# A mask added by a product and six modulation chunks moved to VectorE, in an attention and MLP layer

## The chip, the core and the metric

The kernel runs on one core of a Trainium2 chip. The metric is the device time of one execution in microseconds (us), taken as the median of several runs. In the profile, TensorE's products are rows of PE and its weight loads rows of PEld; VectorE is DVE, ScalarE is ACT, GpSimd is POOL, and SP is the queue that issues most transfers.

## What is computed

One transformer layer on 256 positions of width 2048, in float32, for one sequence. What matters here, cut from the reference:

```python
mod = silu(c) @ mod_w + mod_b                      # 2048 x 12288, a single row
sh_m, sc_m, g_m, sh_f, sc_f, g_f = split(mod, 6)
h = x * (1 + sc_m) + sh_m
q, k, v = split(h @ w_qkv + b_qkv)                 # 32 query heads, 8 key/value heads of 64
s = (rope(q) @ rope(k).T) * 64 ** -0.5
s = where(abs(kpos - qpos) <= 128, s, -inf)
m = maximum(max(s), sink)
p = exp(s - m); p = p / (sum(p) + exp(sink - m))
x = layer_norm(alpha * x + (1 + g_m) * ((p @ v) @ w_o + b_o))
h = x * (1 + sc_f) + sh_f
y = square(relu(h @ w1 + b1)) @ w2 + b2
x = layer_norm(alpha * x + (1 + g_f) * y)
```

With 256 positions there are two query blocks t of 128. Each sees both key blocks. In its own key block nothing is masked. In the other one the window of 128 cuts a triangle off: so the mask has one corner of 128 x 128 that isn't all zero for each t.

## The kernel before

**Numbers.** Full-precision products are made of three products of rounded float32 (float32r): high x high, high x low, low x high (`mm3`, lines 561 to 564; three such products are called a triple below). So every weight tile is loaded once (`raw`, 1 MB), rounded by ScalarE to its high part (`wh`, line 300), and VectorE subtracts to get the low part (`wl`, line 251). Scores, transposes and values are done in plain float32, which the trace shows as two instructions for each product.

**Stages.** The weights stream in the order of their use. First comes the projection to q, k and v (up to some 160 us), beside it the modulation's first part. Then comes the attention stage (`for n in range(21)`): sixteen score sets n = 0 to 15. A set is four query heads of one query block t (n = 4j + 2t + rh). In iteration n the kernel issues the scores of set n, the values of an earlier pair of sets, and a block of weight products: the last parts of q, k and v for small n, then the output projection (`project`). Inside the block stand the transposes of the probabilities of set n - 1 (`probs_T`) and the normalising of set n. Then comes the MLP, which is most of the span and which the change doesn't touch.

**A score set** (`scores`, line 758). Four products of 256 columns (line 775) go to two PSUM banks, two heads in each. VectorE runs `tensor_tensor_reduce` once for each head (line 782): it adds the mask's 256 columns, changes the sign, writes that back to PSUM and reduces the minimum, with the negated sink as the start, into a column of `nm`. In the trace each is a CUSTOM_DVE_ANT_0 and a short DVE_READ_ACCUMULATOR2_ANT. A small addition makes `es` for the sink's term (line 786). ScalarE takes the exponential of each head, with sums (line 791). The mask is written once by GpSimd (`masks`, line 122), as two pieces of 256 columns.

**Modulation.** A chunk is 1 MB of the modulation's weights (`Mod.step`). It goes one of two ways. On TensorE it is `quad`s (line 364): products whose fixed operand has 32 equal columns of the conditioning vector, four of them in the four 32-wide column strips. A chunk of the gate (`m_gm`, width 512) is four products of 512 columns, a chunk of `m_ff` (width 256) eight of 256. On VectorE it is two multiply-adds over 1024 columns (line 404; the first of a group is line 402), into two tiles (for `m_ff`, two into one tile). At a group's end the VectorE part is reduced by four products with ones (line 364, in = `onesf`) on top of TensorE's part. Which chunks go where is written by hand: the lists behind `m_mix`, `m_ff` and `m_gm` (lines 469 to 472).

**What sets the order.** The loads' order and the pace are tables. Within them a scheduler orders the instructions of each engine by the priorities in `AHEAD`, so a change of work moves other instructions too. Once built, each engine runs its queue in order.

Of the kernel before, what the change touches and what calls it, by code (L numbers as in the profile page):

```python
# [21 lines left out]
NT = S // 128  # L22
NK = D // 128
# [6 lines left out]
NEG = -1.0e30  # L30
# [3 lines left out]
FFG = (4, 4, 4, 4)  # L34
# [28 lines left out]
def hybrid_kernel(ctx: ExitStack, tc: tile.TileContext, a, out: bass.AP):  # L63
    nc = tc.nc
    cst = ctx.enter_context(tc.tile_pool(name="cst", bufs=1))
# [38 lines left out]
    onesf = cst.tile([128, 128], F32, name="onesf")  # L104
    nc.vector.memset(onesf, 1.0)
    nc.vector.tensor_copy(onesr, onesf)
    eps = cst.tile([128, 1], F32, name="eps")
    nc.vector.memset(eps, LN_EPS)
    both = cst.tile([128, 2], F32, name="both")
# [10 lines left out]
    fixed = sml.tile([128, 1024], F32, name="sc", bufs=1)  # L120

    def masks():
        msk = fixed[:, :512].rearrange("p (t k) -> p t k", t=NT)
        nc.gpsimd.memset(msk, 0.0)
        nc.gpsimd.affine_select(out=msk[:, 0, 128:], in_=msk[:, 0, 128:], compare_op=OP.is_ge, fill=NEG, base=0,
                                pattern=[[-1, 128]], channel_multiplier=1)
        nc.gpsimd.affine_select(out=msk[:, 1, :128], in_=msk[:, 1, :128], compare_op=OP.is_ge, fill=NEG, base=0,
                                pattern=[[1, 128]], channel_multiplier=-1)
        return msk


    def rotary_tables():
# [327 lines left out]
    def groups(src, sizes, dves):  # L460
        out, c0, k0 = [], 0, 0
        for nk, dve in zip(sizes, dves):
            n = 2 * nk
            out.append((Mod([src[c0 + i] for i in range(n)], 64 * nk, dve), k0, nk))
            c0 += n
            k0 += nk
        return out

    m_mix = groups(a["modm"], MIXG, [(), (), (), (), (1,), (), (0, 4, 5, 6, 7), (3, 5, 6)])
    m_ff = groups(a["modf"], FFG, [(0, 3, 4, 7), (0, 1, 3, 4, 5, 6), (3, 4), (0, 1, 2, 3, 4, 5, 6, 7)])  # L470
    m_gm = Mod([a["modgm"][i] for i in range(NK)], 512, (3, 4, 5, 7, 9, 10, 12, 14), a["modgmb"])
    m_gf = Mod([a["modgf"][i] for i in range(NK)], 512, range(NK), a["modgfb"])

    scm = cst.tile([128, NK], F32, name="scm")
# [208 lines left out]
    for tok in STEPS.split():  # L683
        n = int(tok[1:])
        if tok[0] == "v":
            S.vecs(n)
        elif tok[0] == "i":
            idle(n)
        elif tok[0] == "p":
            S.pace = n  # L690
        elif tok[0] == "n":
            S.nh = n
        elif tok[0] == "l":
            S.nl = n
        elif tok[0] == "M":
            modulated(n)
            if n == 0:
                msk = masks()
# [62 lines left out]
    def scores(n):  # L761

        j, rh, t = n // 4, n % 2, n % 4 // 2

        def of(x):
            return x.rearrange("p (g r i) -> p g r i", r=2, i=2)[:, 2 * j:2 * j + 2, rh]

        pss = [psa.tile([128, 512], F32, name="pa").rearrange("p (i k) -> p i k", i=2) for _ in range(2)]
        nm = sml.tile([128, 4], F32, name="nm")
        for i in range(2):  # L770
            x = (2 * rh + i) * 256 + t * 128
            for s in range(2):
                p = slice(64 * s, 64 * s + 64)
                with first("scores"):
                    nc.tensor.matmul(pss[s][:, i], qT[j][p, x:x + 128], kT[p, j * 256:j * 256 + 256],  # L775
                                     start=True, stop=True)
        with first("softmax"):
            for s in range(2):

                for i in range(2):  # L780
                    h = 4 * (2 * j + s) + 2 * rh + i
                    nc.vector.tensor_tensor_reduce(out=pss[s][:, i], in0=pss[s][:, i], in1=msk[:, t], scale=-1.0,
                                                   scalar=nsnk[:, h:h + 1], op0=OP.add, op1=OP.min,
                                                   accum_out=nm[:, 2 * s + i:2 * s + i + 1])
            es = sml.tile([128, 4], F32, name="es")
            nc.vector.tensor_tensor(es.rearrange("p (s i) -> p s i", s=2), nm.rearrange("p (s i) -> p s i", s=2),
                                    of(snk), op=OP.add)
            P = g4()
            sm = sml.tile([128, 4], F32, name="sm")
            for r in range(4):  # L790
                nc.scalar.activation(P[:, r * 256:r * 256 + 256], pss[r // 2][:, r % 2], AF.Exp, scale=-1.0,
                                     bias=nm[:, r:r + 1], accum_out=sm[:, r:r + 1])
            nc.scalar.activation(es, es, AF.Exp)
        PS[n] = P, sm, es
# [188 lines left out]
    for n in range(21):  # L983
        j, i = n // 4, n % 4
# [574 lines left out]
```

## Time and profile before

| | us |
|---|---|
| median of 3 runs (lowest, highest) | 1066.85 (1065.62, 1068.74) |
| span of the profiled execution | 1064.5 |
| its time in the list of runs | not given on its own; the lowest run is 1065.62 |
| TensorE busy with products | 1051.1 |
| VectorE busy | 964.0 |
| ScalarE busy | 625.4 |

Read it so: the share of busy time is an average over stages. TensorE's rows overlap, since one product starts before the end of the one before it, so the cost of a product is the distance to the next start. Buffer numbers are left out of names: `pa`, `pt` and `pm` are PSUM banks, `g` and `g4b` general tiles of 1024 columns. The granted clock of TensorE is 1.000 for the execution.

### The profile page before, as it was taken

To read this page: it belongs to the slowest core of one execution; us is meant where nothing else is said; L and a number is where in the kernel's file an instruction comes from. 1 tells how busy PE (TensorE), PEld (TensorE's weight loads), DVE (VectorE), ACT (ScalarE), POOL (GpSimd) and SP (SyncE) were. 2 spreads that over 40 slices of the span, in tenths; PEclk is the share of its full clock that TensorE was granted. 3 is DMA by queue.
4 is the path that set the end of the run, shared out by engine and by line. 5 is a ranking of instruction groups with operands and counts; after the bars stand their busy time and mean duration, and the time that the engine had idled before them with its cause. 6 is when DMAs were issued, how large, how long until landed. Compare 5 with 4: busy or idle time off the path is not lost.

```text
span 1064.5 us, 16048 instructions
## 1 busy us (share of the span) xinstructions
PE 1051.1 (99%) x6172; PEld 854.8 (80%) x6172; DVE 964.0 (91%) x1448; ACT 625.4 (59%) x986; POOL 27.6 (3%) x54
## 2 busy tenths in 40 slices
PE   9999899999999999999999999999999999999998
PEld 7677677666677899988888888888888888888886
DVE  4689899989999898999989999899899997999998
ACT  5433347776772637664367777447777446777740
POOL 1000000001000000000000000000000001000000
PEclk9999999999999999999999999999999999999999
DMA  9999997799965897538945654974564793465742
GB/s 383 425 423 426 426 427 300 286 384 354 393 244 199 330 383 294 219 121 312 384 176 194 237 187 171 358 312 163 194 237 164 285 358 136 164 237 200 251 182 79
DMA packets 43516, 292.72 MB, mean 275 GB/s; under 512 B 5152, under 2 KB 5280, under 8 KB 9648
## 3 DMA queue, kind: packets, MB, share of 16 engines
q1 hardware_dynamic: 39456, 279.85, 67.5%
q0 software_dynamic: 3232, 10.50, 3.1%
q10 hardware_dynamic: 752, 1.35, 0.4%
q8 instruction: 48, 0.79, 0.3%
q14 instruction: 28, 0.23, 0.1%
HBM read 289.57 MB, written 2.11 MB: 274 GB/s over the span
## 4 chain that ended last, share of the span: by engine, by line
PE 94%; DVE 3%; ACT 1%; DMA 1%; issue 0%; DVEq 0%; ACTq 0%
PE pa L1195 17%; PE pa L562 15%; PE pa L564 15%; PE pa L563 15%; PE pa L1197 9%; PE pm L364 4%; PE pa L1169 3%; PE pa L1168 3%; PE pa L1167 3%; PE pa L775 2%; PE pt L564 2%; PE pt L563 2%; PE pt L562 2%; PE pa L836 1%; PE pt L819 1%; PE pa L672 1%
## 5 line engine op out<-in xcount | busy, mean ns | idle before, releaser
L300 ACT CAST wh<-raw 128x1024 fp32r<-128x1024 f32 (+1 forms) x332 | 333.8, 1016 | 251.0 <-PE pa L564 100.2
L251 DVE TENSOR_TENSOR wl<-raw,wh 128x1024 fp32r<-128x1024 f32 (+1 forms) x332 | 386.0, 1177 | 47.4 <-ACT wh L300 44.1
L562 PE MATMUL pa<-wh,g 128*128 128x512 f32 (+1 forms) x611 | 242.8, 399 | 4.8 <-ACT g L585 4.8
L563 PE MATMUL pa<-wl,g 128*128 128x512 f32 (+1 forms) x611 | 238.1, 390 | 0.0
L564 PE MATMUL pa<-wh,g 128*128 128x512 f32 (+1 forms) x611 | 237.3, 390 | 0.2 <-DVE g L587 0.2
L1195 PE MATMUL pa<-g,wh 128*128 128x512 f32 x768 | 191.5, 391 | 0.0
L1195 PEld LDWEIGHTS pa<-g,wh 128*128 128x128 f32 x768 | 140.6, 188 | 28.2 <-issue 0.8
L562 PEld LDWEIGHTS pa<-wh,g 128*128 128x128 f32 x611 | 114.7, 188 | 41.1 <-ACT g L585 6.4
L564 PEld LDWEIGHTS pa<-wh,g 128*128 128x128 f32 x611 | 114.7, 188 | 26.5 <-issue 1.6
L563 PEld LDWEIGHTS pa<-wl,g 128*128 128x128 f32 x611 | 114.9, 188 | 23.0 <-DVE scm L445 0.4
L1197 PEld LDWEIGHTS pa<-g,wl 128*128 128x128 f32 x768 | 104.8, 190 | 7.5
L1197 PE MATMUL pa<-g,wl 128*128 128x256 f32 x768 | 107.1, 282 | 0.0
L404 DVE SCALAR_TENSOR_TENSOR g<-raw,cact,g 128x1024 f32<-128x1024 f32 (+1 forms) x69 | 86.2, 1257 | 0.8 <-DMA raw<-in_modm 0.4
L1167 PE MATMUL pa<-g,wh 128*128 128x256 f32 x240 | 67.8, 285 | 0.2 <-ACT wh L300 0.2
L1169 PE MATMUL pa<-g,wh 128*128 128x256 f32 x240 | 67.6, 285 | 0.0
L1168 PE MATMUL pa<-g,wl 128*128 128x256 f32 x240 | 67.5, 285 | 0.0
L251 DVE TENSOR_TENSOR raw<-raw 128x1024 fp32r<-128x1024 f32 x54 | 65.6, 1221 | 0.0
L300 ACT CAST raw<-raw 128x1024 fp32r<-128x1024 f32 x54 | 56.0, 1045 | 8.2 <-DVE raw L262 4.4
L1168 PEld LDWEIGHTS pa<-g,wl 128*128 128x128 f32 x240 | 45.8, 192 | 0.7 <-issue 0.4
L1167 PEld LDWEIGHTS pa<-g,wh 128*128 128x128 f32 x240 | 45.9, 192 | 0.5 <-ACT wh L300 0.4
L1169 PEld LDWEIGHTS pa<-g,wh 128*128 128x128 f32 x240 | 45.8, 192 | 0.1
L605 DVE TENSOR_TENSOR g<-g,pa 128x512 f32<-128x512 f32 x60 | 39.3, 682 | 6.9 <-PE pa L564 6.6
(250 smaller groups left out, 1364.0 us busy)
## 6 DMA issues: line engine op xcount, KB each, us to landing
raw<-in_w1b SPq DMA_DIRECT2D x48, 1024.0 KB, 6.8
raw<-in_modm SPq DMA_DIRECT2D x32, 1024.0 KB, 12.6
raw<-in_modf SPq DMA_DIRECT2D x32, 1024.0 KB, 7.0
raw<-in_w SPq DMA_DIRECT2D x32, 1024.0 KB, 7.2
raw<-in_w2s SPq DMA_DIRECT2D x27, 1024.0 KB, 5.6
raw<-in_wqkv SPq DMA_DIRECT2D x24, 1024.0 KB, 14.2
raw<-in_modgm SPq DMA_DIRECT2D x16, 1024.0 KB, 7.3
raw<-in_wo SPq DMA_DIRECT2D x16, 1024.0 KB, 7.3
```

The lines of the kernel that those rows point to most:

```text
L251: self.pinned(nc.vector.tensor_sub(l[:, :w], r, f32(self.hs[n])[:, :w]))
L300: self.pinned(nc.scalar.copy(h[:, :s.shape[-1]], s))
L364: i = nc.tensor.matmul(self.ps[32 * j:32 * j + 32, :w], lhsT[j] if type(lhsT) is list else lhsT, rhs[j], start=self.first, stop=stop)
L404: nc.vector.scalar_tensor_tensor(p[:, :e], s, cact[:, kt:kt + 1], p[:, :e], op0=OP.mult, op1=OP.add)
L562: nc.tensor.matmul(ps, xh, wh, start=start, stop=False)
L563: nc.tensor.matmul(ps, xh, wl, start=False, stop=False)
L564: S.prev = nc.tensor.matmul(ps, xl, wh, start=False, stop=stop).ins
L1167: nc.tensor.matmul(o, wh(w, 128), hh, start=new, stop=False)
L1168: nc.tensor.matmul(o, wl(w, 128), hh, start=False, stop=False)
L1169: nc.tensor.matmul(o, wh(w, 128), hl, start=False, stop=end)
L1195: nc.tensor.matmul(ps, wh(k, 128), ff_in(k), start=k == 0, stop=False)
L1197: nc.tensor.matmul(ps[:, :256], wl(k, 128), ff_in(k)[:, :256], start=False, stop=k == NK - 1)
```

## The change

The mask's corner is now stored rounded, beside a rounded identity matrix, in a new tile `rounded`. ScalarE makes the two copies, next to the start of the kernel. In each score set, two products with the identity (one for each bank, 2 x 128 columns) add the corner onto the half of the scores that it belongs to, for both heads of the bank at once. VectorE then takes one maximum over 256 scores for the two heads of a bank (`tensor_reduce`, negated), so two instructions in a set instead of four, and a small one combines all four with the negated sink. Scores are no longer written back by VectorE, and their sign stays, so the exponential's scale of -1 goes.

Six more modulation chunks are summed on VectorE: one each of `m_ff`'s first two groups, and chunks 6, 11, 13 and 15 of the gate `m_gm`. To make room in SBUF, the buffer for GpSimd's transfer descriptors is set to 8192 bytes.

```diff
+    rounded = cst.tile([128, 512], F32R, name="rounded")
...
     def masks():
-        msk = fixed[:, :512].rearrange("p (t k) -> p t k", t=NT)
-        nc.gpsimd.memset(msk, 0.0)
-        nc.gpsimd.affine_select(out=msk[:, 0, 128:], in_=msk[:, 0, 128:], compare_op=OP.is_ge, fill=NEG, base=0,
-                                pattern=[[-1, 128]], channel_multiplier=1)
...
+        corner = fixed[:, :256].rearrange("p (t k) -> p t k", t=NT)
+        nc.gpsimd.memset(corner, 0.0)
+        for t, step in enumerate((-1, 1)):
+            nc.gpsimd.affine_select(out=corner[:, t], in_=corner[:, t], compare_op=OP.is_ge, fill=NEG, base=0,
+                                    pattern=[[step, 128]], channel_multiplier=-step)
+        nc.scalar.copy(rounded[:, :256], fixed[:, :256])
+        nc.scalar.copy(rounded[:, 256:384], ident)
+        return rounded[:, :256].rearrange("p (t k) -> p t k", t=NT), rounded[:, 256:384]
...
-    m_ff = groups(a["modf"], FFG, [(0, 3, 4, 7), (0, 1, 3, 4, 5, 6), (3, 4), (0, 1, 2, 3, 4, 5, 6, 7)])
-    m_gm = Mod([a["modgm"][i] for i in range(NK)], 512, (3, 4, 5, 7, 9, 10, 12, 14), a["modgmb"])
+    m_ff = groups(a["modf"], FFG, [(0, 2, 3, 4, 7), (0, 1, 2, 3, 4, 5, 6), (3, 4), (0, 1, 2, 3, 4, 5, 6, 7)])
+    m_gm = Mod([a["modgm"][i] for i in range(NK)], 512, (3, 4, 5, 6, 7, 9, 10, 11, 12, 13, 14, 15), a["modgmb"])
...
                     nc.tensor.matmul(pss[s][:, i], qT[j][p, x:x + 128], kT[p, j * 256:j * 256 + 256],
-                                     start=True, stop=True)
+                                     start=i == 0, stop=False)
+        far = slice(128 - 128 * t, 256 - 128 * t)
+        for s in range(2):
+            with first("scores"):
+                nc.tensor.matmul(pss[s][:, :, far], eye, msk[:, t, None, :].to_broadcast([128, 2, 128]),
+                                 start=False, stop=True)
         with first("softmax"):
             for s in range(2):
-
-                for i in range(2):
-                    h = 4 * (2 * j + s) + 2 * rh + i
-                    nc.vector.tensor_tensor_reduce(out=pss[s][:, i], in0=pss[s][:, i], in1=msk[:, t], scale=-1.0,
-                                                   scalar=nsnk[:, h:h + 1], op0=OP.add, op1=OP.min,
-                                                   accum_out=nm[:, 2 * s + i:2 * s + i + 1])
+                nc.vector.tensor_reduce(out=nm[:, 2 * s:2 * s + 2], in_=pss[s], axis=AX.X, op=OP.max, negate=True)
             es = sml.tile([128, 4], F32, name="es")
-            nc.vector.tensor_tensor(es.rearrange("p (s i) -> p s i", s=2), nm.rearrange("p (s i) -> p s i", s=2),
-                                    of(snk), op=OP.add)
+            nm3 = nm.rearrange("p (s i) -> p s i", s=2)
+            nc.vector.tensor_tensor(nm3, nm3, of(nsnk), op=OP.min)
+            nc.vector.tensor_tensor(es.rearrange("p (s i) -> p s i", s=2), nm3, of(snk), op=OP.add)
...
-                nc.scalar.activation(P[:, r * 256:r * 256 + 256], pss[r // 2][:, r % 2], AF.Exp, scale=-1.0,
+                nc.scalar.activation(P[:, r * 256:r * 256 + 256], pss[r // 2][:, r % 2], AF.Exp,
                                      bias=nm[:, r:r + 1], accum_out=sm[:, r:r + 1])
...
-    nc = bacc.Bacc("TRN2", target_bir_lowering=False, num_devices=1)
+    nc = bacc.Bacc("TRN2", target_bir_lowering=False, num_devices=1, dynamic_dma_scratch_size=8192)
```

The scheduler moves other instructions too. Two places matter to the prediction. In the new kernel the line numbers are higher by two or three.

The first place is VectorE's queue at score set 5. Before, with `pa` the scores, `nm` the maxima, `g_1524` and `g_1525` the two halves of the gate's sum:

```order
L840 TENSOR_TENSOR g_1896<-pa,g_1895 128x512
L782 ISA pa,nm<-pa,sc,nsnk 128x256
L782 ISA nm 128x1
L782 ISA pa,nm<-pa,sc,nsnk 128x256
L782 ISA nm 128x1
L782 ISA pa,nm<-pa,sc,nsnk 128x256
L782 ISA nm 128x1
L782 ISA pa,nm<-pa,sc,nsnk 128x256
L782 ISA nm 128x1
L251 TENSOR_TENSOR wl<-raw,wh 128x1024
L786 TENSOR_TENSOR es<-nm,pack 128x4
L404 SCALAR_TENSOR_TENSOR g_1524<-raw,cact,g_1524 128x1024
```

Before set 5, the value remainder (line 840) stands ahead of the scores' instructions. Now, the same engine and place, where `g_1527` and `g_1528` are the gate's sum:

```order
L406 SCALAR_TENSOR_TENSOR g_1527<-raw,cact,g_1527 128x1024
L786 TENSOR_REDUCE nm<-pa 128x2 x2
L843 TENSOR_TENSOR g_1900<-pa,g_1899 128x512
L789 TENSOR_TENSOR nm<-nm,nsnk 128x4
L406 SCALAR_TENSOR_TENSOR g_1528<-raw,cact,g_1528 128x1024
L790 TENSOR_TENSOR es<-nm,pack 128x4
L253 TENSOR_TENSOR wl<-raw,wh 128x1024 x2
L406 SCALAR_TENSOR_TENSOR g_1527<-raw,cact,g_1527 128x1024
L406 SCALAR_TENSOR_TENSOR g_1528<-raw,cact,g_1528 128x1024
L803 TENSOR_TENSOR rs<-sm,es 128x4
```

Two maxima stand where four pairs stood. Other work (a value remainder, a chunk's half) stands between the maxima and the small instructions that depend on them, and more chunk halves follow.

The second place is TensorE's queue between score sets 6 and 7, at the end of the gate's group. `pm` is the modulation's bank. Before, first the gate's last chunk with its reduction, and then, four triples later, the values and scores:

```order
L562 MATMUL pa<-wh,g_1895 128x512
L563 MATMUL pa<-wl,g_1895 128x512
L564 MATMUL pa<-wh,g_1896 128x512
L364 MATMUL pm<-raw,cact 32x512 x4
L364 MATMUL pm<-g_1524,onesf 32x512 x2
L364 MATMUL pm<-g_1525,onesf 32x512 x2
L819 MATMUL pt<-ident,g_2104 128x128 x8
```

The reduction follows directly on the last chunk, as one run of eight 32-wide products. The values and scores of the same iteration:

```order
L564 MATMUL pa<-wh,g_1896 128x512
L364 MATMUL pm<-raw,cact 32x256 x16
L836 MATMUL pa<-g_2158,g_330 64x512 x2
L836 MATMUL pa<-g_2159,g_330 64x512 x2
L775 MATMUL pa<-g_1589,g_1963 128x256 x4
L562 MATMUL pa<-wh,g_1895 128x512
```

They are runs of sixteen, four and four. Now the same engine and place:

```order
L566 MATMUL pa<-wh,g_1900 128x512
L839 MATMUL pa<-g_2161,g_333 64x512 x2
L366 MATMUL pm<-g_1527,onesf 32x512 x2
L839 MATMUL pa<-g_2162,g_333 64x512
L366 MATMUL pm<-g_1528,onesf 32x512 x2
L839 MATMUL pa<-g_2162,g_333 64x512
L777 MATMUL pa<-g_1592,g_1968 128x256 x2
L366 MATMUL pm<-raw,cact 32x256 x8
L777 MATMUL pa<-g_1592,g_1968 128x256 x2
L782 MATMUL pa<-rounded 128x2x128 x2
L822 MATMUL pt<-ident,g_2218 128x128 x8
```

The reduction has moved in among the value products, in two pieces, and eight modulation products stand in the middle of the scores. The new corner products (line 782 there) close the score set.

More of the change, by code (lines that the diff above doesn't have):

```diff
@@ L122, in masks @@
     def masks():
-        msk = fixed[:, :512].rearrange("p (t k) -> p t k", t=NT)
-        nc.gpsimd.memset(msk, 0.0)
-        nc.gpsimd.affine_select(out=msk[:, 0, 128:], in_=msk[:, 0, 128:], compare_op=OP.is_ge, fill=NEG, base=0,
-                                pattern=[[-1, 128]], channel_multiplier=1)
-        nc.gpsimd.affine_select(out=msk[:, 1, :128], in_=msk[:, 1, :128], compare_op=OP.is_ge, fill=NEG, base=0,
-                                pattern=[[1, 128]], channel_multiplier=-1)
-        return msk
+        corner = fixed[:, :256].rearrange("p (t k) -> p t k", t=NT)
[6 more added lines that the diff above has]
+        return rounded[:, :256].rearrange("p (t k) -> p t k", t=NT), rounded[:, 256:384]
     def rotary_tables():
@@ L697, in hybrid_kernel @@
             if n == 0:
-                msk = masks()
+                msk, eye = masks()
             if n == 2:
```

## The prediction

> **What bounds the kernel now.** I read the page first: the span, the engines' shares and the chain that ended last.
>
> ```profile
> span 1064.5 us, 16048 instructions
> PE 1051.1 (99%) x6172; PEld 854.8 (80%) x6172; DVE 964.0 (91%) x1448; ACT 625.4 (59%) x986; POOL 27.6 (3%) x54
> PE 94%; DVE 3%; ACT 1%; DMA 1%; issue 0%; DVEq 0%; ACTq 0%
> ```
>
> TensorE is on the chain for 94% of the span, so what the change puts on or takes off its queue counts almost fully, if TensorE gets what it waits for on time. VectorE, at 91%, is the engine that could fail to deliver. Where the change lies in time is told by line 782, the mask-and-maximum instruction that it removes (its view gives durations min/median/max, first and last start). The next rows are the busy time of each engine in that stretch (columns: stretch, length, then PE, PEld, DVE, ACT and POOL with counts, granted clock, DMA share, GB/s), and VectorE's for line 782 alone.
>
> ```profile
> L782 DVE CUSTOM_DVE_ANT_0 pa<-pa,sc,nsnk x64: 460/488/494, 165.0 to 309.8; 128x256 f32<-128x256 f32 x64
> 163.00:310.00 147.00, 146.84 (x863) 99.80 (x863) 139.87 (x292) 109.23 (x274) 9.03 (x14) 1.00 0.87 338
> 163.00:310.00 147.00, 28.30 (x127) 1.00 0.87 338
> ```
>
> TensorE has 0.2 us without work, at full clock. VectorE has 7.1 us without work in 147, and 28.3 us of its time is line 782. The waits in the attention stage say who waits for whom:
>
> ```profile
> PE pt L753 <- ACT g L822: 0.2, 1, 0.2
> DVE pa L782 <- PE pa L775: 2.4, 4, 1.3
> ACT g L791 <- DVE nm L782: 21.4, 13, 3.4
> ```
>
> TensorE waits 0.2 us in all. VectorE keeps up, and part of its idle time is waiting for TensorE's scores. So this stage is TensorE's, with VectorE 5% behind: a change that gives both engines something and takes something from both.
>
> **Term 1, TensorE: six chunks leave.** A stretch of TensorE's timeline holds every kind of product that the sum needs (start us, us, what; a next start minus a start is what a row costs, since ends overlap).
>
> ```profile
> 205.10 0.39 PE L563 MATMUL pa<-wl,g 128*128 128x512 f32 x1
> 205.33 0.39 PE L564 MATMUL pa<-wh,g 128*128 128x512 f32 x1
> 205.65 1.06 PE L364 MATMUL pm<-raw,cact 128*32 128x512 f32 x8
> 206.64 1.94 PE L836 MATMUL pa<-g,g 128*64 128x512 f32 x8
> 208.51 1.13 PE L775 MATMUL pa<-g,g 64*128 64x256 f32 x8
> 209.57 1.06 PE L364 MATMUL pm<-raw,cact 128*32 128x512 f32 x8
> 210.57 0.50 PE L562 MATMUL pa<-wh,g 128*128 128x512 f32 x1
> 210.90 0.39 PE L563 MATMUL pa<-wl,g 128*128 128x512 f32 x1
> ...
> 217.13 1.13 PE L775 MATMUL pa<-g,g 64*128 64x256 f32 x8
> ...
> 222.99 1.09 PE L819 MATMUL pt<-ident,g 128*128 128x128 f32 x8
> 223.84 0.48 PE L562 MATMUL pa<-wh,g 128*128 128x512 f32 x1
> ```
>
> A plain product starts 0.23 us after the one before it (205.10 to 205.33). A chunk of line 364 takes 0.99 to 1.00 us (205.65 to 206.64, 209.57 to 210.57). Going from plain products to 32-column ones costs 0.32 instead of 0.23, and the second plain product behind such a stretch starts 0.33 after the first: about 0.1 us for each change of tile shape. Six chunks of 1.0 us leave; most stand beside other tiled products, so that few shape changes leave with them. I take -6.0 us, from -5.6 to -6.6 (where a chunk stands between plain products, two changes go too).
>
> **Term 2, TensorE: 32 corner products come.** Each has 256 columns in one rounded pass, the shape of line 1197 in the chain:
>
> ```profile
> 542.67 0.95 PE pa L1197 x8
> ```
>
> 0.95 / 8 = 0.119 us each, so 32 x 0.119 = +3.8 us. The shape change behind the scores is paid today by the plain product there, so it is not added again. Lower end: if the first of each pair fits into that change, 16 x 0.1 less, +2.2. Upper end: the corner product writes two runs of 128 columns with a gap of 128, and no row shows a product with gaps; the nearest dearer row is a score product of 256 columns, 1.06 / 4 = 0.265 us (208.51 to 209.57), which gives +8.5. I take +3.8, since the rounded 256-column row is the same work. [...]
>
> **Term 3, TensorE: the new order.** With the gate's chunk 15 on VectorE, the gate's last reduction (four products of ones) is issued between the value products of set 5: two value products, two reductions, one value, two reductions, one value, then two scores, eight modulation products, two scores. Before, these were runs of four or eight. The durations by shape show why runs matter:
>
> ```profile
> L836 PE MATMUL pa<-g,g 128*64 128x512 f32 x64 | 15.5, 605 | 0.0
> L364 PE MATMUL pm<-raw,cact 128*32 128x512 f32 x64 | 8.5, 604 | 0.0
> L563 PE MATMUL pa<-wl,g 128*128 128x512 f32 x603 | 235.8, 391 | 0.0
> ```
>
> A full-precision instruction of 512 columns lasts 0.60 us in both narrow shapes, although eight start within 1.87 us in one and within 0.99 in the other: two value products, or four chunk products, run side by side. Alone, one takes about as long as its pair or set: a pair of value products 1.87 / 2 = 0.93, a lone one 0.93 too, a pair of reductions about 0.9 where a set of four takes 0.99. So 0.93 + 0.9 + 0.93 + 0.9 + 0.93 = 4.6 in place of 1.87 + 0.99 = 2.9, +1.7, and some four more shape changes at 0.1: +2.1, of which the part for lone products is the uncertain one. Lower end +0.4 (they overlap all the same). I take +2.0. The probability transposes of four sets are split by a plain triple, and the scores of set 15 stand inside its value products: some three shape changes more, +0.3 (0 to 0.5).
>
> TensorE in sum: -6.0 + 3.8 + 2.0 + 0.3 = **+0.1 us**. The intended exchange (-6.0 + 3.8) is a gain of 2.2, and the order takes it back.
>
> **Term 4, VectorE.** Its timeline gives the prices:
>
> ```profile
> 181.08 0.49 DVE L782 CUSTOM_DVE_ANT_0 pa<-pa,sc,nsnk 128x256 f32<-128x256 f32 x1
> 181.49 0.49 DVE L782 CUSTOM_DVE_ANT_0 pa<-pa,sc,nsnk 128x256 f32<-128x256 f32 x1
> ...
> 182.30 1.22 DVE L251 TENSOR_TENSOR wl<-raw,wh 128x1024 fp32r<-128x1024 f32 x1
> 183.44 0.16 DVE L786 TENSOR_TENSOR es<-nm,pack 128x4 f32<-128x4 f32 x1
> 183.51 2.48 DVE L404 SCALAR_TENSOR_TENSOR g<-raw,cact,g 128x1024 f32<-128x1024 f32 x2
> 185.90 0.16 DVE L800 TENSOR_TENSOR rs<-sm,es 128x4 f32<-128x4 f32 x1
> ...
> 187.19 1.25 DVE L605 TENSOR_TENSOR g<-g,pa 128x512 f32<-128x512 f32 x2
> 188.37 1.22 DVE L251 TENSOR_TENSOR wl<-raw,wh 128x1024 fp32r<-128x1024 f32 x1
> ```
>
> The removed instruction costs 0.41 us from start to start, four in a set 1.6, and 28.3 us in the stretch by the row above. A chunk half of line 404 costs (185.90 - 183.51) / 2 = 1.195, a small one 0.07 (183.44 to 183.51). A maximum over 512 scores isn't in the trace. The nearest row that reads 512 columns of PSUM is line 605, (188.37 - 187.19) / 2 = 0.59; the bound above is two of the removed ones, 0.81. I take 0.60, near line 605: it reads as many columns of PSUM, and what it writes is next to nothing. [...]
>
> A set's maximum now costs 2 x 0.60 + 0.1 = 1.3, sixteen 20.8 to 22 with their gaps: 6.3 to 7.5 saved, say 6.6. The six chunks add 12 x 1.195 = 14.3. Net +7.7, and all twelve halves stand between the first and the last score set in the new order. So VectorE would need 139.9 + 7.7 = 147.6 us of a stretch of 147. Its idle time was the cover for everything it does, and it is gone.
>
> Does that reach TensorE at once? The queue gives some room. From the maxima of set 5 to those of set 6 VectorE has two maxima, three halves, three low parts (1.14, 182.30 to 183.44), five 512-column ones (a value remainder, two rope products, two evictions, at 0.6) and small ones: 1.2 + 3.6 + 3.4 + 3.0 + 0.3 = 11.5 us, while TensorE comes from set 5 to set 6 in 7.9 (8.6 before, from 208.51 to 217.13, less a chunk, plus the corner). VectorE then trails by 3.6. The gate's reduction, which now waits for chunk 15, stands behind eight triples of plain products (8 x 0.68), eight transposes (0.85, from 222.99 to 223.84) and two values (0.93), 7.2 us after set 6; the tile that it reads first is ready some 3.6 + 3.7 = 7.3 after set 6 (two maxima, a low part, a small one and a half chunk). That is even to within half a microsecond: a new wait of nothing to 1, with two values and set 7's scores queued behind it on TensorE. Low parts for the weights stand about one block ahead in the new order, so they have more room. I take +1.0 for all waits (0 to 4).
>
> ```profile
> 0.00:60.00 60.00, 55.99 (x564) 41.55 (x565) 35.81 (x69) 28.86 (x43) 4.97 (x16) 1.00 0.98 406
> ```
>
> ScalarE's two more copies stand in this stretch, where ScalarE has 31 us to spare and the DMA engines are busy 98% of the time: 0 (0.5 if the weights' casts slip). The exponentials already wait 21.4 us for VectorE, so ScalarE isn't late by itself: 0. The smaller descriptor buffer touches only GpSimd's transfers, and all DMA is 1% of the chain: 0.
>
> **The sum** is +0.1 + 1.0 = +1.1: a span of 1065.6 where the profiled execution had 1064.5. The median of the runs shown, 1066.85, lies 2.35 above that span; with the same offset the forecast is **1068.0 us**.
>
> **Rivals.** Bounds: 0.3% is 3.2 us, about what a measurement of this kernel can tell from no change.
>
> 1. *VectorE becomes the bound* (slower). If a maximum costs 0.68 or more rather than 0.60, VectorE needs 147.6 + 32 x 0.08 = 150.2 us in the stretch; with the 1 us of waits for scores that can't be filled, TensorE is held by some 4: 1066.85 + 0.1 + 4 = 1071. It decides from about 0.65 per maximum on, or where the gate's reduction waits over 2 us. For it: 147.6 against 147. Against it: trailing costs nothing until a buffer is empty, and the idle time after the last set takes some back. Chance 0.25.
> 2. *The corner products are slow* (slower): 0.265 us in place of 0.119, +4.7 more, 1072.7. For it: nothing here writes with gaps. Against it: runs of 128 columns are long, and the rounded row that I take has the same number of columns. Chance 0.05. [...]
> 3. *The exchange pays* (faster): the corner's first product hides in the shape change (+2.2), the mixed products overlap (+0.4), chunks take their shape changes along (-6.6), splits +0.2, no wait: -3.8, 1063.0. For it: VectorE had 7 us to spare and TensorE is 94% of the chain. Against it: the shapes above. Chance 0.15.
>
> That the change does nothing it says can't be: the instructions are in the order.
>
> **The numbers.** The forecast has 0.55; its own range is 1064.7 to 1069.6 (removal -6.6 to -5.6, order 0.4 to 2.1, waits 0 to 2). With rival 1 reaching to 1071 and half of rival 3, 1063 to 1072 leaves out less than 2 in 10. Faster by over 0.3% is rival 3, 0.15; slower rivals 1 and 2, 0.30; the same 0.55.
>
> **What would show it.** Line 364 with 512 columns: 32 fewer instructions, some 4 us less. The corner line: 32 products, two of them 0.24 us behind the scores (0.5 if rival 2 holds). A maximum: 0.60 from start to start; VectorE's busy time in the stretch of the score sets 146 or more. Around the gate's reduction TensorE spends some 4.6 us on four values and four reductions, with a wait for line 404's tile under 1 us. Wrong would be: no TensorE wait and a shorter stretch by over 3 us, or waits for the low parts (line 251) or for the normalised probabilities that sum to more than 3.

## The result, and the profile after

The changed kernel takes **1079.55 us** (median of 4 runs, 1078.97 to 1081.32) beside 1067.3 for the kernel before (4 runs). The ratio is 1.0121, with an interval of 1.0106 to 1.0135, so the change costs about 13 us. The forecast was 1068.0, with a range from 1063 to 1072: wrong, and on the slower side. Three executions among all the runs of this document (1746.59 us of e3, 1485.24 of e13 and 4794.42 of the kernel before) lasted far longer than the others of their kernels, and the ratios are taken without them.

The profiled execution of the changed kernel is the longest of its four (1081.32 us; its span is 1079.5, those of the other three are 1077.2 to 1078.2). Sums below are made against its span, 15.0 above that of before. The page first:

```profile
span 1079.5 us, 15948 instructions
PE 1059.6 (98%) x6140; PEld 861.7 (80%) x6140; DVE 972.6 (90%) x1380; ACT 625.0 (58%) x988; POOL 27.2 (3%) x54
PE 84%; DVE 10%; ACT 3%; DMA 2%; issue 1%; DVEq 0%; ACTq 0%
```

TensorE's share of the chain fell from 94 to 84%, and VectorE's rose from 3 to 10%. So the kernel now waits for VectorE's and ScalarE's results in places where it did not. Where these places are is read from TensorE's timeline: the first score set, and the filler products that open the turn-over to the MLP. After:

```profile
169.97 1.13 PE L777 MATMUL pa<-g,g 64*128 64x256 f32 x8
364.13 0.96 PE L674 MATMUL pa<-onesr 128*128 128x512 f32 x3
```

And the same two places before:

```profile
163.21 1.14 PE L775 MATMUL pa<-g,g 64*128 64x256 f32 x8
348.77 0.96 PE L672 MATMUL pa<-onesr 128*128 128x512 f32 x3
```

So 6.8 us are lost before the first score set, where the prediction had 0; 194.2 - 185.6 = 8.6 in the attention stage; and the MLP takes 715.4 where it took 715.7. These are the 15.0.

**In front.** ScalarE's timeline of the changed kernel, where `rounded<-sc` is the new copy of the mask's corner, line 302 casts weights to their high part, and line 587 shifts and scales the first block of activations:

```profile
12.34 0.41 ACT L129 CAST rounded<-sc 128x256 fp32r<-128x256 f32 x1
12.64 2.00 ACT L302 CAST wh<-raw 128x1024 fp32r<-128x1024 f32 x2
16.85 1.99 ACT L302 CAST wh<-raw 128x1024 fp32r<-128x1024 f32 x2 [2.21 <-DMA raw<-in_wqkv]
18.75 0.59 ACT L587 ACTIVATE g<-g,shm,scm 128x256 fp32r<-128x256 f32 x1
```

Before, the shift stood ahead of the casts:

```profile
11.77 0.60 ACT L585 ACTIVATE g<-g,shm,scm 128x256 fp32r<-128x256 f32 x1
12.27 1.99 ACT L300 CAST wh<-raw 128x1024 fp32r<-128x1024 f32 x2
```

The shift came 7 us later, because it now stands behind a pair of casts that wait for a transfer. TensorE's first products need it:

```profile
19.39 1.21 PE L564 MATMUL pa<-wh,g 128*128 128x512 f32 x4 [1.94 <-ACT g L587]
21.44 0.79 PE L565 MATMUL pa<-wl,g 128*128 128x512 f32 x1 [0.83 <-DVE wl L253]
22.03 0.63 PE L566 MATMUL pa<-wh,g 128*128 128x512 f32 x1
22.46 0.63 PE L565 MATMUL pa<-wl,g 128*128 128x512 f32 x1
```

It stands idle for 1.94 and 0.83 us, and then a plain product takes 0.43 us (22.03 to 22.46) where it takes 0.23 at a granted clock of 1.00 (23.16 to 23.39 in the kernel before). The granted clock (the third number from the end) shows the same:

```profile
20.00:25.00 5.00, 4.17 (x11) 2.97 (x10) 4.79 (x5) 0.00 (x0) 0.00 (x0) 0.56 1.02 428
25.00:30.00 5.00, 5.00 (x18) 3.82 (x17) 0.00 (x0) 2.61 (x5) 0.00 (x0) 0.75 1.01 426
55.00:60.00 5.00, 5.00 (x43) 3.60 (x42) 5.00 (x8) 1.05 (x1) 0.00 (x0) 0.68 1.01 423
250.00:255.00 5.00, 5.00 (x22) 3.64 (x21) 3.19 (x4) 2.07 (x5) 0.00 (x0) 0.72 1.01 423
```

The third row is a second drop in front, after a wait of 1.64 us near 52 that the kernel before has as well (near 45) and passes at a clock of 1.00 in its profiled execution. Together the drops in front cost at most 5 x (0.44 + 0.25 + 0.32) = 5.0 us of work. The last row is another such place, in the attention stage.

**In the attention stage.** TensorE waited 0.2 us here before. Now it is 5.1, most of it these:

```profile
PE pt L755 <- ACT g L825: 2.9, 2, 2.4
PE pa L564 <- DVE g L607: 1.1, 1, 1.1
PE pa L777 <- ACT g L757: 0.8, 1, 0.8
```

The longest wait follows set 7, whose scores start at 237.16. VectorE then (line 786 is the maximum, 789 the small minimum with the negated sink):

```profile
241.58 1.27 DVE L786 TENSOR_REDUCE nm<-pa 128x2 f32<-128x512 f32 x2
242.77 1.21 DVE L253 TENSOR_TENSOR wl<-raw,wh 128x1024 fp32r<-128x1024 f32 x1
243.90 0.15 DVE L789 TENSOR_TENSOR nm<-nm,nsnk 128x4 f32<-128x4 f32 x1
```

On ScalarE, the copies of the transposed probabilities (line 825) are queued behind the exponentials (line 794):

```profile
244.26 1.06 ACT L302 CAST wh<-raw 128x1024 fp32r<-128x1024 f32 x1 [3.86 <-PE pa L566]
245.22 0.46 ACT L794 ACTIVATE g<-pa,nm 128x256 f32<-128x256 f32 x1
248.06 1.09 ACT L825 COPY g<-pt 128x512 f32<-128x512 f32 x2
```

TensorE waits for those copies to free a PSUM bank before it can go on:

```profile
248.71 1.51 PE L755 MATMUL pt<-ident,g 128*128 128x128 f32 x8 [2.45 <-ACT g L825]
250.14 2.08 PE L777 MATMUL pa<-g,g 64*128 64x256 f32 x8
```

The exponentials start 245.22 - 237.16 = 8.1 us after the scores. Before it was 2.6, by the timelines of TensorE, VectorE and ScalarE at set 7: VectorE got to the scores 1.2 us after they had started, and the exponentials came 1.4 after that.

```profile
230.50 1.13 PE L775 MATMUL pa<-g,g 64*128 64x256 f32 x8
231.66 0.49 DVE L782 CUSTOM_DVE_ANT_0 pa<-pa,sc,nsnk 128x256 f32<-128x256 f32 x1 [1.25 <-PE pa L775]
233.06 0.47 ACT L791 ACTIVATE g<-pa,nm 128x256 f32<-128x256 f32 x1 [1.86 <-DVE nm L782]
```

Three things hold them up. The maximum begins 4.4 us after the scores' start: the scores, with modulation products and the corner among them, take until 239.9, and VectorE is then at a chunk half and a sum of the output projection until 241.58. Between the maximum and the minimum stands a low part of 1.13 us (242.77 to 243.90) that has nothing to do with the set: the scheduler fills the gap between two dependent instructions with whatever is ready. Before, the sink was the start value of the one instruction, and there was no such gap. And on ScalarE a weight cast stands ahead of the exponentials and waits 3.86 us for TensorE. The minimum is ready at 243.90 + 0.15 = 244.05; the exponentials start at 245.22, when the cast is out of the way. So at set 7 it is the order of ScalarE's queue that sets their start in the end, as at sets 2, 4 and 12; in seven other sets they wait for the minimum itself.

A ledger of TensorE's time from set 0 to the turn-over puts a size to each part. It is worked out from the timeline of each profiled execution: the start of a row to the start of the next one, less the idle time shown, summed by kind of product, to about 0.1 us. The columns e2 to e12 are experiments below; "exp" is the mean time from a set's first score to its first exponential over sets 2 to 13, from the same timelines.

| us | before | after | e2 | e4 | e5 | e6 | e7 | e11 | e12 |
|---|---|---|---|---|---|---|---|---|---|
| set 0 at | 163.2 | 170.0 | 165.0 | 163.7 | 163.5 | 163.5 | 164.0 | 163.7 | 163.2 |
| stage | 185.6 | 194.2 | 194.4 | 195.3 | 192.9 | 189.0 | 190.7 | 194.2 | 187.4 |
| idle | 0.2 | 5.1 | 5.4 | 3.8 | 6.3 | 2.9 | 1.1 | 5.7 | 1.0 |
| chunks | 14.5 | 8.8 | 8.8 | 14.5 | 8.9 | 8.9 | 14.5 | 8.9 | 10.8 |
| corner | 0 | 5.9 | 5.6 | 5.7 | 0 | 5.5 | 5.5 | 5.5 | 5.5 |
| plain triples | 121.2 | 119.6 | 119.5 | 119.8 | 121.6 | 119.4 | 119.7 | 122.6 | 119.7 |
| reductions | 2.1 | 3.1 | 3.1 | 2.1 | 3.1 | 2.1 | 2.1 | 2.1 | 2.1 |
| values | 15.0 | 16.2 | 16.3 | 15.3 | 15.9 | 15.9 | 15.0 | 15.9 | 14.9 |
| scores, transposes | 32.6 | 35.5 | 35.8 | 34.1 | 37.2 | 34.3 | 32.8 | 33.5 | 33.3 |
| exp | 3.16 | 5.42 | 5.47 | 5.05 | 4.81 | 3.94 | 3.38 | 3.71 | 3.27 |

### The profile page after: what moved, and what is told of

Read it like the earlier page. It is cut to its first block, busy times and chain, and to the rows that moved or that the text cites. A ratio compares the mean times of both kernels' runs of the same rounds, so it can differ in the third digit from the quotient of the medians.

```text
span 1079.5 us, 15948 instructions
## 1 busy us (share of the span) xinstructions
PE 1059.6 (98%) x6140; PEld 861.7 (80%) x6140; DVE 972.6 (90%) x1380; ACT 625.0 (58%) x988; POOL 27.2 (3%) x54
## 4 chain that ended last, share of the span: by engine, by line
PE 84%; DVE 10%; ACT 3%; DMA 2%; issue 1%; DVEq 0%; ACTq 0%
PE pa L1198 16%; PE pa L564 13%; PE pa L566 13%; PE pa L565 13%; PE pa L1200 8%; PE pm L366 3%; DVE g L406 3%; PE pa L1172 3%; PE pa L1171 2%; PE pa L1170 2%; DVE wl L253 2%; PE pt L566 2%; PE pt L565 2%; PE pt L564 2%; DMA raw<-in_wqkv 1%
## 5 line engine op out<-in xcount | busy, mean ns | idle before, releaser
L406 DVE SCALAR_TENSOR_TENSOR g<-raw,cact,g 128x1024 f32<-128x1024 f32 (+1 forms) x81 | 101.2, 1257 | 0.4
```

Of the source, the lines that this page charges most:

```text
L406: nc.vector.scalar_tensor_tensor(p[:, :e], s, cact[:, kt:kt + 1], p[:, :e], op0=OP.mult, op1=OP.add)
```

## The experiments

The theories that the runs set against each other: **F**, ScalarE's copies cost the time in front; **C**, the larger part of that is TensorE's clock after the idle time; **V**, in the attention stage VectorE has too much to do (rival 1 of the prediction); **L**, the way from scores to exponentials is longer, whatever the load.

### First four: each part alone

The copies alone (e1), in the kernel before (with the smaller descriptor buffer):

```diff
+        nc.scalar.copy(rounded[:, :256], fixed[:, :256])
+        nc.scalar.copy(rounded[:, 256:384], ident)
         return msk
```

> The kernel before, with only the tile, ScalarE's two rounded copies and the smaller descriptor buffer added; the copies' result is not used. Theory F (the copies push the first block's shift on ScalarE behind four weight casts, TensorE waits about 2.8 us near 20 us, its clock drops and the next products cost another 4 us): set 0 starts about 6.8 us later than before, time about 1073.5. Rival (the copies cost nothing, the loss ahead of set 0 comes from the chunks or from run to run): set 0 at 163, time about 1067.

Measured: 1070.58, ratio 1.0044 (1.0026 to 1.0061). TensorE's timeline has the same wait as the changed kernel:

```profile
19.50 1.20 PE L565 MATMUL pa<-wh,g 128*128 128x512 f32 x4 [2.01 <-ACT g L588]
```

Set 0 starts at 170.1, and the stage behind it takes 185.5, as before. F holds for the place and the cause. The size by the medians is 4 us and not 6.8: the profiled execution, at 1072.32, is one of the longer ones, and five runs range from 1069.47 to 1074.44.

The copies on VectorE (e2), in the changed kernel:

```diff
-        nc.scalar.copy(rounded[:, :256], fixed[:, :256])
-        nc.scalar.copy(rounded[:, 256:384], ident)
+        nc.vector.tensor_copy(rounded[:, :256], fixed[:, :256])
+        nc.vector.tensor_copy(rounded[:, 256:384], ident)
```

> The changed kernel with the two rounded copies on VectorE, which puts the first shift ahead of the casts again. Theory F: no clock below 1 in the first 60 us, set 0 starts at about 163.2, and the time falls by 6.8 to about 1072.8; the 8 us lost from set 7 on stay. Rival (the loss in front is not the copies'): 1079.5.

Measured: 1075.77, ratio 1.0080 (1.0063 to 1.0097), 0.0041 or 4.4 us below the changed kernel's ratio. The shift is ahead of the casts again:

```profile
11.91 0.60 ACT L587 ACTIVATE g<-g,shm,scm 128x256 fp32r<-128x256 f32 x1
12.41 1.99 ACT L302 CAST wh<-raw 128x1024 fp32r<-128x1024 f32 x2
```

The wait near 19 us is gone, and the stage is as long as in the changed kernel (194.4). So the two losses stand apart from each other. Set 0 starts at 165.0 and not at 163.2. The mean granted clock of this execution is 0.996, where the profiled execution of before has 1.000; where ahead of set 0 the 1.8 us were lost isn't shown.

The mask by product alone (e4), with the copies on VectorE and the chunks' lists as before:

```diff
-    m_ff = groups(a["modf"], FFG, [(0, 2, 3, 4, 7), (0, 1, 2, 3, 4, 5, 6), ...
-    m_gm = Mod(..., 512, (3, 4, 5, 6, 7, 9, 10, 11, 12, 13, 14, 15), a["modgmb"])
+    m_ff = groups(a["modf"], FFG, [(0, 3, 4, 7), (0, 1, 3, 4, 5, 6), ...
+    m_gm = Mod(..., 512, (3, 4, 5, 7, 9, 10, 12, 14), a["modgmb"])
```

> The new mask and maximum alone, with the copies on VectorE and the six chunks back on TensorE. Theory V (VectorE is overfilled by the chunks, and trails from set 5 on): VectorE has 6.6 us less to do than before, TensorE waits for the copies of the transposed probabilities under 1 us, and the time is that of before plus the corner products at 0.34 us a set: about 1072. Rival L (the chain of a set is longer by the small minimum, which the scheduler puts behind another instruction of about 1.1 us, so that the exponentials start late whatever the load): TensorE still waits 2.5 us or more in the attention stage, 1075 or more.

Measured: 1074.68, ratio 1.0074 (1.0059 to 1.0089). TensorE waits 3.8 us; the two longest waits are:

```profile
PE pa L839 <- ACT g L825: 1.2, 1, 1.2
PE pa L564 <- DVE g L607: 1.1, 1, 1.1
```

And yet VectorE (the third busy time) is far from full. Its row for 186 us from about set 0 on:

```profile
163.00:349.00 186.00, 182.00 (x1043) 126.16 (x1042) 163.76 (x252) 123.56 (x299) 9.03 (x14) 1.00 0.80 300
```

The same 186 us of the kernel before:

```profile
163.00:349.00 186.00, 185.84 (x1087) 130.02 (x1087) 175.18 (x346) 123.94 (x300) 9.03 (x14) 1.00 0.80 303
```

It is busy for 11.4 us less in as long a stretch, and over the whole stage, which is longer here, for 172.8 of 195.2 us where it was 174.8 of 185.6. Yet TensorE waits 3.7 us more. V can't explain that; L can: the exponentials come 5.05 us after the scores, where it was 3.16.

The six chunks alone (e5): the same four lines the other way round, in the kernel before, with its old mask instruction.

> The six chunks alone on VectorE (and the smaller descriptor buffer), with the old mask instruction. Theory V: VectorE needs 139.9 + 14.3 = 154.2 us in a stretch of 147, so TensorE is held by 7 or more, less the 6 us of products that leave: 1068 to 1074, with waits for VectorE's results of several us. Rival L (the longer chain of the new maximum is the cause, not the load): waits under 1 us, and 6 us of products less with some 2 for the order: about 1063. If the smaller descriptor buffer were what costs in front, set 0 would start 6.8 us late here too; theory F says 163.2.

Measured: 1073.84, ratio 1.0070 (1.0052 to 1.0087). Set 0 starts at 163.5, so the smaller descriptor buffer costs nothing in front. The stage loses 7.4 us, and these are the two longest waits:

```profile
PE pt L753 <- ACT g L822: 1.7, 1, 1.7
PE pa L562 <- DVE g L605: 1.2, 1, 1.2
```

Its row for the same 186 us:

```profile
163.00:349.00 186.00, 179.52 (x956) 123.33 (x955) 181.47 (x346) 124.46 (x299) 9.03 (x14) 1.00 0.80 303
```

VectorE is busy for 181.5 of 186. At sets 6 and 7 it gets to the scores 7.4 and 8.7 us after they started. So V is real too, when the chunks come without a cheaper maximum. Neither theory alone explains the changed kernel, which has 176.6 us of VectorE work in as long a stretch (170 to 356), hardly more than before.

### Four more: the small minimum, the clock, fewer chunks

In e6 and e7, and in e11 and e12 that build on e6, the exponent is shifted by the maximum of the scores alone, without the sink; the softmax is the same as long as the sink's exponential doesn't overflow. The edit of e6, on top of e2:

```diff
-            nc.vector.tensor_tensor(nm3, nm3, of(nsnk), op=OP.min)
```

> The changed kernel with the copies on VectorE and without the small minimum with the negated sink: the exponent is shifted by the maximum of the scores alone, so the exponentials follow the maximum directly. Theory L (the longer way from the scores to the exponentials costs): mean time from a set's scores to its first exponential falls from 5.2 to about 4.0 us, and half or more of the 7 us that e2 lost within the attention stage come back: about 1072. Theory V (only VectorE's load counts): the small instructions are 16 x 0.07 = 1.1 us of VectorE's time, and the time stays within 1 us of e2's, 1075 to 1076.

Measured: 1069.5, ratio 1.0035 (1.0023 to 1.0047), 0.0045 or 4.8 us below e2's ratio, for sixteen instructions of 0.07 us. The waits fall from 5.4 to 2.9, the clock drop of the attention stage goes (a granted clock of 1.00 from 163 to 349 us, 0.99 in e2), and the way to the exponentials is 3.94. Most of the waits left are these:

```profile
PE pt L755 <- ACT g L824: 1.8, 3, 0.8
```

Two things become shorter at once. The gap ahead of the minimum goes. And the exponentials of the first bank no longer wait for the second bank's maximum, since the minimum combined all four heads. At set 7 they now start 0.73 us after the first of the two maxima, before the second is done:

```profile
234.78 1.30 DVE L786 TENSOR_REDUCE nm<-pa 128x2 f32<-128x512 f32 x2
235.51 0.47 ACT L793 ACTIVATE g<-pa,nm 128x256 f32<-128x256 f32 x1 [2.59 <-DVE nm L786]
```

Of the 5.4 us by which the stage is shorter than e2's, 2.5 are waits and 1.5 scores and transposes, most of that the lower clock (the scores behind e2's wait of 2.45 took 1.92, the same ones here 1.06); 1.0 is the gate's reduction, which stands in one run again. So the new order has a part in the gain, and no run separates the gap from the first bank's wait.

The same edit on top of e4 (e7), so with the chunks as before:

> The new mask and maximum alone (chunks as before, copies on VectorE), without the small minimum. Theory L: TensorE's 3.8 us of waits in the attention stage go to under 1.5, time about 1071.5, which is that of before plus the corner products (3.9 net of a shape change that they take over). Rival (the waits come from somewhere else than the way to the exponentials): waits stay at 3 to 4 us, time 1074 to 1075.

Measured: 1072.29, ratio 1.0056 (1.0041 to 1.0071). One wait is left, for an eviction of the modulation:

```profile
PE pm L366 <- ACT mrow L423: 1.1, 1, 1.1
```

So in the traces L holds with and without the chunks: 2.5 and 2.7 us of waits go. In the times it is clear with them (0.0045) and not without: 0.0018 from e4 to e7, with intervals that overlap. What remains of the mask by itself is mostly the products: 5.5 us in the ledger, less 1.5 that the triples behind the scores save.

Now the clock in front (e3): the changed kernel with more filler products at the wait.

```diff
-STEPS = 'v1 i4 n4 v1 i13 l4 M0 i4 n4 l3 i4 f1 ...
+STEPS = 'v1 i4 n4 v1 i13 l4 M0 i4 n4 l3 i16 f1 ...
```

> The changed kernel with twelve more of the filler products of ones (0.23 us each, 2.7 us in all) where TensorE waits for the first shift near 19 us. The wait itself stays. Theory C (the larger part of the 6.8 us in front is TensorE's clock, which drops after that idle time): no clock below 1 between 20 and 30 us, set 0 starts at about 166 to 167 in place of 170, time about 1076. Rival (the wait alone counts, the clock is an effect without a price): set 0 still at 170, 1079.5.

Measured: ratio 1.0121 (1.0093 to 1.0149), from times that lie far apart: 1076.89, 1077.67 and 1082.34. In the profiled execution (1076.89) the drop is gone:

```profile
20.00:25.00 5.00, 3.74 (x19) 2.73 (x16) 4.54 (x6) 0.39 (x1) 0.00 (x0) 1.00 1.01 423
```

Set 0 starts at 167.0, 3.0 earlier. So it was run once more, below.

Three chunks on VectorE in the kernel before (e9: gate's 6 and 11, one of `m_ff`):

```diff
+    m_ff = groups(a["modf"], FFG, [(0, 2, 3, 4, 7), (0, 1, 3, 4, 5, 6), ...
+    m_gm = Mod(..., 512, (3, 4, 5, 6, 7, 9, 10, 11, 12, 14), a["modgmb"])
```

> The kernel before with three of the six chunks on VectorE (gate's 6 and 11, one of the first group of the MLP's modulation), old mask and maximum. Theory V with half the load: VectorE has 7.2 us more to do where 7 were free; three chunks of 0.96 us leave TensorE. If the idle time can be used: 1063.5 to 1065. If trailing at sets 6 and 7 costs as in the six-chunk run, waits of 1 to 3 us eat it: 1066 to 1068.

Measured: 1069.81, ratio 1.0035 (1.0024 to 1.0046), slower than either expectation. TensorE's idle time in the stage is 3.2 us, and what the three chunks free (2.9) is spent on values and transposes, which stand in more and shorter runs (+1.0 and +1.5).

### The last four

The edit of e3 once more (e10):

> The changed kernel with twelve more filler products once more, for its time, since one run of the first try stood far outside the others. Theory C: set 0 at about 167 and a time of 1076 to 1077.5, 2 to 3.5 less than the changed kernel's 1079.55. Rival: 1079 or more.

Measured: 1079.86, ratio 1.0125 (1.0109 to 1.0142), no better than the changed kernel. Set 0 starts at 168.6, and the clock is 1.00 from 20 to 30 us, but it drops later, after the wait of 1.64 us, as in the changed kernel:

```profile
50.00:55.00 5.00, 3.19 (x9) 1.92 (x8) 4.67 (x8) 1.55 (x2) 0.00 (x0) 0.82 1.00 419
```

By the times, the rival to C holds: removing that one drop doesn't make the kernel measurably faster. But the edit did more than fill TensorE's wait. In both executions with it the second pair of casts got its transfer later (it starts at 17.90 and 18.05, where it was 16.85), so that TensorE's first product came at 20.45 and 20.60 instead of 19.39 and gave back over 1 us; whether the filler products are the cause isn't shown. The mean granted clock of the four runs is 0.997 to 1.000 here and 0.993 to 0.996 in the changed kernel, some 3 us of work, and the time is the same. So what the drop costs isn't settled by these two runs.

e11: as e6, with the maxima at a higher priority:

```diff
+ ('attention', 'softmax'): 100,
```

> As e6 (copies on VectorE, no small minimum, six chunks), with a higher priority for the maxima in the attention stage, so that fewer chunk halves and low parts stand between and ahead of them. Theory L: the mean time from scores to the first exponential falls below e6's 3.87, the waits below 2.9, 1067.5 to 1069. Theory V (at sets 6 and 7 VectorE simply has more to do than TensorE takes time): the late maxima at sets 6 and 7 (6 us) stay late, waits move to the low parts or the value remainders, 1069 to 1071.

Measured: 1070.51, ratio 1.0045 (1.0030 to 1.0060), no gain over e6. The maxima of sets 6 and 7 come 3.0 and 2.7 us after the scores instead of 6.0 and 5.5. But another result is late for it in the profiled execution, a sum of the output projection:

```profile
PE pa L564 <- DVE g4b L953: 4.0, 1, 4.0
```

V expected the time and that the waits would move, and was wrong that the maxima would stay late. L expected the shorter way (3.71 us) and was wrong on waits and time. So it fits that the work at sets 6 and 7 is too much and the order chooses who waits. But this execution (1074.84; after the wait of 4.0, plain products start 0.43 apart from 237.59 to 241.43) is the longest of six, and the others took 1069.74 to 1070.78; whether they had the same wait isn't on record.

e12: as e11, with the gate's chunks 13 and 15 back on TensorE:

```diff
+    m_gm = Mod(..., 512, (3, 4, 5, 6, 7, 9, 10, 11, 12, 14), a["modgmb"])
```

> As e11, with the gate's chunks 13 and 15 back on TensorE, which takes 4.7 us off VectorE around sets 5 to 8. TensorE has 1.9 us more products than with six. Theory V: the maxima of sets 6 and 7 come within 3 us, waits below 1 us, 1066 to 1068, no more than e11. Theory L alone: nothing gained from a lighter VectorE, 1.9 us more than e11.

Measured: 1069.56, ratio 1.0033 (1.0017 to 1.0049). In the profiled execution (1067.92) the idle time is 1.0 us, and the stage 187.4 in place of 194.2, so V's step is seen there, though the time is above the 1066 to 1068 that V expected. The six runs range from 1067.75 to 1072.51, and the ratios of e11 and e12 overlap: in the median no difference between the two is shown.

One chunk alone (e13: gate's 6) in the kernel before:

```diff
+    m_gm = Mod(..., 512, (3, 4, 5, 6, 7, 9, 10, 12, 14), a["modgmb"])
```

> The kernel before with the gate's chunk 6 alone moved to VectorE, old mask. In the three-chunk run the sets after that chunk stood 1.2 us earlier than before until chunk 11 came. If VectorE's idle time takes this one chunk: about 1 us less than before, 1064.8. If even one chunk makes the maxima late: 1066 or more.

Measured: 1068.02, ratio 1.0017 (1.0007 to 1.0026). Even one chunk moved is no gain. Its 0.9 us leave TensorE, and the values of one pair of sets, now issued as two and six instead of eight, take 1.0 more. No kernel tried here beats the one before.

## Why the prediction was wrong, point by point

- **The chunks (term 1): right.** -6.0 forecast, 14.5 - 8.8 = 5.7 measured.
- **The corner products (term 2): right, and rival 2 falls.** The stretch at set 0 shows the pair and the first plain products behind it:

```profile
171.03 0.51 PE L782 MATMUL pa<-rounded 128*128 128x256 f32 x2
171.38 0.39 PE L565 MATMUL pa<-wl,g 128*128 128x512 f32 x1
171.60 0.39 PE L566 MATMUL pa<-wh,g 128*128 128x512 f32 x1
```

  The pair takes 0.35, of which 0.1 is the shape change that the plain product had paid. In the ledger that is 5.9 - 1.6 = 4.3 net, 3.8 forecast; some 0.25 of it is the pair that ran at the lower clock near 252. The two runs of 128 columns with a gap cost nothing that can be seen: without the shape change the pair takes 0.25, where 2 x 0.119 = 0.24 was forecast.
- **The new order (term 3): right for the values and reductions, short for the rest.** The values mixed with reductions take 237.16 - 232.19 = 5.0, where 4.6 was forecast in place of 2.9:

```profile
232.19 1.08 PE L839 MATMUL pa<-g,g 128*64 128x512 f32 x4
233.19 1.05 PE L366 MATMUL pm<-g,onesf 128*32 128x512 f32 x4
...
236.16 1.07 PE L839 MATMUL pa<-g,g 128*64 128x512 f32 x2
```

  TensorE's own work in the stage grew by 194.2 - 5.1 - 185.4 = 3.7, with +0.1 forecast. Close to 2 of it are the products that ran at the lower clock around 250, right after the wait of 2.45 (the scores there took 2.0 instead of 1.06). About 1 more is that transposes and scores stand in more pieces (25 and 17 runs in the stage instead of 22 and 16), where 0.3 was forecast for all splits.
- **The maximum (in term 4): right.** 241.58 to 242.77 is 1.19 for two, 0.595 each, with 0.60 forecast.
- **VectorE's load: right in size.** Its busy time over the whole execution rose by 8.6; net +7.7 was forecast. It is spread over a longer stage, though: in the first 147 us from set 0 on (170 to 317) VectorE is busy for 141.4, where the sum had 147.6.
- **The waits (in term 4): this step failed.** +1.0 was forecast, from 0 to 4; it was 5.1 - 0.2 = 4.9, and behind the longest of them the clock dropped (0.72 from 250 to 255 us). The working took the set's maximum as "2 x 0.60 + 0.1" and asked only whether VectorE's queue is full. It did not see that the 0.1 is a second step on the way to the exponentials, and that the scheduler puts another instruction ahead of it in 13 of the 16 sets, such as the low part of 1.13 us at set 7. The order that the document itself shows at set 5 has that row: a value remainder between the maxima and line 789. Nor did it see that a step which combines all four heads makes the first bank's exponentials wait for the second bank's maximum. e6 and e7 show it: without the step the waits fall by 2.5 and 2.7.
- **ScalarE's copies: this step failed too.** "0 (0.5 if the weights' casts slip)" was argued from idle time in the stretch. But what counts is what the queue's order becomes: the first shift slipped behind the casts, not the casts behind the copies. It cost 6.8 us in the profiled execution, about 4.4 by the ratios of e2 and the changed kernel.
- **The descriptor buffer: right.** e5 has it, and set 0 starts at 163.5.
- **The gate's reduction: right that the wait is nothing.** It is not in the list of waits.
- **Rival 1** named the right direction and a part of the mechanism. Its 1071 lacked both failed steps. Its point of decision, a maximum above 0.65 or a late reduction, was not what decided.

By ratios the loss of 0.0121 divides so: 0.0041 from the copies (e2), 0.0045 from the minimum (e6), and 0.0035 that is left in e6, where the stage is 3.5 us longer than before with 2.7 of that in waits, 2.1 of them at and around sets 6 and 7. That this rest is VectorE's load is shown in kind by e5, less surely by e11, and in size only by the profiled execution of e12.

What stays open: how much of the loss in front is clock and how much is wait. In the changed kernel's profiled execution the waits near 20 us are 2.8 and the drops at most 5.0, while a wait of 2.15 near 114 that the kernel before has is gone. The profiled executions with the filler products reach set 0 by 3.0 and 1.4 us earlier, the times show nothing. Whether keeping the copies on ScalarE but fixing the shift's place would cost anything was not tried.

## What to carry to other kernels

When one fused instruction becomes a cheaper one and a tiny one, price the tiny one by what the scheduler may put in front of it, and follow the chain through to the engine that waits at its end: 0.07 us of work cost some 5 here. Ask as well whether it makes parts wait for each other that were independent. "The engine has room" is an argument about its load and not about its order; for every instruction added to a queue, look at who moved behind whom at the first place where something waits. And an exchange of a few microseconds between two engines that are both busy over 90% is decided by these second-order terms, so it should be sized against them first.

## What the runs showed of the hardware

TensorE's clock dropped after some short idle times, and not after others. After 1.94 and 0.83 us of idle time within 4 us, plain products took 0.43 us instead of 0.23, about half the speed. By the rows from 20 to 30 us that lasted 5 x (0.44 + 0.25) / 0.5 = 6.9 us. After 2.45 us near 248 it was about 3 us (0.72 from 250 to 255). A wait of 2.15 us near 114 in the kernel before had no drop behind it (1.00 from 110 to 125). The wait of 1.64 us near 46 is in the kernel before at full clock:

```profile
45.00:50.00 5.00, 3.50 (x24) 2.39 (x28) 4.67 (x8) 1.46 (x3) 0.00 (x0) 1.00 1.00 419
```

The same stretch of e4, with the same wait, has a drop:

```profile
45.00:50.00 5.00, 3.19 (x10) 2.00 (x9) 4.67 (x8) 1.55 (x2) 0.00 (x0) 0.80 1.02 426
```

So drops followed waits of 1.64 and 2.45 us, and in the profiled execution of before waits of 1.64 and 2.15 us were followed by none; these runs don't show what decides. At half the clock, drops of 3 to 7 us are 1.5 to 3.5 us of lost work, an estimate from the rows above: a wait of some 2 us on TensorE was followed by the loss of about as much again in one execution, and by no loss in another.
